# First FFN projection: products added in PSUM, two tiles begun together, differences on VectorE

## The chip, the cores and the metric

The kernel runs on one core of a Trainium2 chip (trn2). A core has a matrix engine (TensorE, PE in the profile; its weight loads are PEld), three engines for elementwise work (VectorE, DVE; ScalarE, ACT; GpSimd, POOL), SyncE (SP), which here issues most DMAs, and DMA engines. The engines run side by side, each through its own queue in order, and wait for each other on semaphores. The metric is the device time of one execution in microseconds (us); lower is better.

## What is computed

The reference is one encoder layer in float32: windowed attention with 16 heads over 2048 tokens of width 1024, then a SwiGLU feed-forward network (FFN) with a hidden width of 2816, each between norms and gates. The stage that the change edits is the first line of the FFN:

```python
def swiglu(h, w_in, w_out):
    a, b = jnp.split(h @ w_in, 2, axis=-1)
    return (jax.nn.silu(a) * b) @ w_out
```

## The kernel before

**Stages.** Attention comes first, then from about 780 us on the first FFN projection (`h @ w_in`, silu, product), from about 1645 us the second (`@ w_out`), with the last norm and gate at the end. Results of the first projection go to DRAM and are read back by the second.

**Precision.** Every float32 operand is split into a high and a low half (`split`, L149: a cast on ACT writes the high half, L150; a subtraction on DVE writes the low one, L151), and each product is three matmuls (`three`, L143: high x high, high x low, low x high).

**Seven products for eight.** The first projection works on two halves of 1024 tokens (`hf`), each two chunks of 512 tokens, and on 22 tiles of hidden columns (`t`), each 128 columns of `a` and the matching 128 of `b`. A tile is a 2 x 2 block product of weights (a11, a12, a21, a22) and tokens (b11, b12, b21, b22), computed in Winograd's form: seven products of sums s1 to s4 of the weights (on POOL, L879 to L882) with sums t1 to t4 of the tokens (made earlier, and read from DRAM). A product (`Block.step`) is 4 steps of depth x 3 = 12 matmuls of 128 x 512 into one PSUM bank; a tile is 84 matmuls. The names in the profile are pc_i for the banks, wa_i and ws_i for the split weights, hb and ht for the split tokens, wiri for the raw weights, s_i for their sums.

**What reads the banks.** The order of products is `STEPS` with `OPERANDS`: b11, t2, b21, t3, t1, t4, b22. Each product has a bank of its own, six banks turn around (`psC`, L825). `Hidden.take` (L939 to L963) reads each bank once, the fifth twice, and adds them up in SBUF tiles: p1 (a copy by ACT, L943), u2, u3, b1 (additions by DVE, L946 to L962). `done` takes the silu of each `a` block on ACT (L968) and multiplies it by its `b` block on POOL (L972).

**Pairs.** After each odd tile `give_pair` writes the two tiles' results to DRAM, with the sums that the second projection needs: two subtractions on POOL (L923, L927), two on DVE (L924, L930). In the second half (`parted`, the parts in `SPLIT`) it splits each result before writing (gh and gl tiles), and its last two tiles are written without sums.

**Around it.** `Operands.load` reads and splits the tokens of a half; four of the seven operands of the first half can be loaded only when the attention's last blocks have freed their memory, the first three earlier. Weights of a tile go through one of two raw tiles (`wi`), and their splits through two rings of 7 (`ww`). `late_h` prepares the tokens of the last chunks (transposes, L659, and differences, L676 to L683) between the tiles of the first half. The last two tiles of each half go product by product in turn (`interleaved`), while the next half's operands, or the second projection's first operands (`first_weights`), are loaded.

**What sets the order.** The framework plans each engine's queue ahead: it goes through the instructions by the order of the program (with a few raised in priority), by their dependences and its own estimate of their times. On the chip an engine then works through its queue in that order, and an instruction that waits holds what stands behind it.

Of the kernel before, what the change touches and what calls it, by code (L numbers as in the profile page):

```python
# [17 lines left out]
P = 128  # L18
# [49 lines left out]
def encoder_layer(ctx, tc, a):  # L68
# [71 lines left out]
    def rot(pl, tag, bufs):  # L140
        return lambda name: pl.tile([P, CH], F32, tag=tag, name=name, bufs=bufs)

    def three(ps, w, h, first=False, last=False):  # L143

        pe.matmul(ps, w[0], h[0], start=first, stop=False)  # L145
        pe.matmul(ps, w[0], h[1], start=False, stop=False)  # L146
        pe.matmul(ps, w[1], h[0], start=False, stop=last)  # L147

    def split(hi, lo, src, eng):  # L149
        act.copy(hi, src)  # L150
# [714 lines left out]

    class Block:

        STEPS = tuple(zip(("a11", "s2", "a12", "s3", "s1", "a22", "s4"), OPERANDS))

        def __init__(self, ops, i, u, wa, wb):  # L870
            self.ops, self.u, m = ops, u, ops.m
# [9 lines left out]
            pool.tensor_tensor(sm_["s3"], a11, a21, ALU.subtract)  # L881
            pool.tensor_tensor(sm_["s4"], a12, sm_["s2"], ALU.subtract)  # L882
            src = dict(sm_, a11=a11, a12=a12, a22=a22)
            self.w = {}
            for e, (n, _) in enumerate(self.STEPS):
                side = int(e >= 3 and ww[1] is not None)
                w = ww[side].tile([P, 2, m, P], F32R, tag="w", bufs=wbufs[side], name=f"w{n}_{u}")
                split(w[:, 0], w[:, 1], src[n], dve)
                self.w[n] = w

        def step(self, i):
            an, bn = self.STEPS[i]
            w, h, m = self.w[an], self.ops.ops[bn], self.ops.m
# [7 lines left out]
    def give_pair(hf, j):  # L901

        b = {f"b{e + 1}{i + 1}": hidden.pop((2 * j + e, i)) for e in range(2) for i in range(CPH)}
        parted = (hf, part_of[hf][j][0]) in SPLIT

        def give(n, t, keep):
            d = g_d[hf][j][n]
            if not parted:
                sp.dma_start(d[:, 0], t)
                return  # L910
            hi = temp(f"gh{hf}_{j}_{n}").bitcast(F32R)
            lo = (temp(f"gl{hf}_{j}_{n}") if keep else t).bitcast(F32R)
# [12 lines left out]
        give("t3", b12, False)  # L925
        give("b22", b22, True)
        pool.tensor_tensor(b22, b22, b11, ALU.subtract)  # L927
        give("t1", b11, False)
        give("b21", b21, True)
        dve.tensor_tensor(b21, b21, b22, ALU.subtract)  # L930
        give("t2", b22, False)
        give("t4", b21, False)

    class Hidden(Block):
        def __init__(self, half, t, hf):
            super().__init__(half, t, f"i{half.u}_{t}", a["w_in"][t], a["w_in"][HT + t])
            self.t, self.got, self.hf = t, {}, hf

        def take(self, i, ps):  # L939
            u = self.u  # L940
            if i == 0:
                self.p1 = temp(f"p1_{u}")
                act.copy(self.p1, ps)  # L943
            elif i == 1:
                self.u2 = temp(f"u2_{u}")
                dve.tensor_tensor(self.u2, ps, self.p1, ALU.add)  # L946
# [18 lines left out]
        def done(self, i, j, v):  # L965

            if i == 0:
                act.activation(v, v, AF.Silu)  # L968
            self.got[i, j] = v
            if (1 - i, j) in self.got:  # L970
                sa, b = self.got[0, j], self.got[1, j]
                pool.tensor_tensor(sa, sa, b, ALU.mult)  # L972
                hidden[self.t, j] = sa
                if self.t % 2 and len(self.got) == 4:
                    give_pair(self.hf, self.t // 2)

    def interleaved(pair, nxt, end=iter(())):
# [10 lines left out]
    def first_weights():  # L988

        raws, m = [], PARTS[0][0]  # L990
        for k in range(m):
            raws.append([hA.tile([P, 2, CH], F32R, tag="b11", name=f"wr0_{k}_{e}") for e in range(2)])
            for e in range(2):
                sp.dma_start(f(raws[k][e]), a["w_out"][2 * k + e].rearrange("p (i c) -> p i c", i=2))
        yield
        for k in range(m):
# [6 lines left out]
        for i in range(2):  # L1003
            for k in range(m):
                t = b21p.tile([P, 2, CH], F32R, tag="b21", name=f"g0_{i}_{k}")
                sp.dma_start(f(t[:, 1]), g_d[0][k][("b21", "t1")[i]][:, 0])
                split(t[:, 0], t[:, 1], f(t[:, 1]), dve)
                first_g[0, 0, i, k] = t
        yield
        for i, n in enumerate(("a12", "s1", "a11")):  # L1010
            for k, src in enumerate(first_src):
                t = t3p.tile([P, 2, CH], F32R, tag="t3" if i < 2 else "t1", name=f"wo0_{n}_{k}")
                split(t[:, 0], t[:, 1], src[n], dve)
                first_w[0, 0, i, k] = t
                if n == "s1":
                    pool.tensor_tensor(src["s2"], src["s1"], src["a11"], ALU.subtract)
                    pool.tensor_tensor(src["s4"], src["a12"], src["s2"], ALU.subtract)
            if i == 1:
                yield
# [37 lines left out]
                        h2_d[hf * CPH + int(n[2]) - 1][:, 2 * k + (n[1] == "2"), :])  # L1057
    half = half_ops(0)
    with tc.high_priority(offset=1):
        half.load("b11", "t2", "b21")  # L1060
    last_blocks(range(LAG, JB))
    held = Hidden(half, 0, 0)
    st0.close()
# [3 lines left out]
    wi[1] = open_pool(ffn, "wi1")  # L1067
    ww[1] = open_pool(ffn, "ww1")
    with tc.high_priority(offset=100):
        half.load("t3", "t1", "t4", "b22")  # L1070
    tmp = open_pool(ffn, "tmp", 10)
    cbp = open_pool(ffn, "cbp", 2)

# [12 lines left out]

    gating = gate()
    for hf in range(S // HALF):
        for t in range(HT - 2):
            hid = Hidden(half, t, hf) if held is None else held  # L1090
            held = None
            for i in range(7):
                hid.step(i)
            next(gating if hf else late, None)
        pair = [Hidden(half, t, hf) for t in range(HT - 2, HT)]
        half = None
        if hf + 1 < S // HALF:
# [71 lines left out]
    class Grams:  # L1169
# [4 lines left out]
        def load(self, n=1):  # L1174
            for _ in range(n):
# [4 lines left out]
                for k in range(PARTS[hf][p]):  # L1180
# [4 lines left out]
                        latest[:] = [sp.dma_start(f(t), d).ins]  # L1185
                    else:
                        latest[:] = [sp.dma_start(f(t[:, 1]), d[:, 0]).ins]
                        split(t[:, 0], t[:, 1], f(t[:, 1]), dve)
                    self.g[hf, p, i, k] = t

    z = {}
# [160 lines left out]
```

## Time and profile before

| | us |
|---|---|
| median of 3 runs | 2087.45 |
| lowest, highest | 2087.05, 2092.54 |
| the profiled execution | 2086.54 |
| its span | 2084.7 |

The span is the stretch from the first to the last instruction that the profile shows. Durations come from this one execution. A row of a timeline gives start, duration, engine, line, operation, output <- input, partitions x elements and count, and in brackets how long the engine was idle before it and what it waited for. A row of waits gives the total in us, the count and the longest. Matmul records last 0.39 us and overlap; their starts tell the rate.

### The profile page before, as it was taken

To read this page: it belongs to the slowest core of one execution; us is meant where nothing else is said; L and a number is where in the kernel's file an instruction comes from. 1 tells how busy PE (TensorE), PEld (TensorE's weight loads), DVE (VectorE), ACT (ScalarE), POOL (GpSimd) and SP (SyncE) were. 2 spreads that over 40 slices of the span, in tenths; PEclk is the share of its full clock that TensorE was granted. 3 is DMA by queue.
4 is the path that set the end of the run, shared out by engine and by line. 5 is a ranking of instruction groups with operands and counts; after the bars stand their busy time and mean duration, and the time that the engine had idled before them with its cause. 6 is when DMAs were issued, how large, how long until landed. Compare 5 with 4: busy or idle time off the path is not lost.

```text
span 2084.7 us, 28731 instructions
## 1 busy us (share of the span) xinstructions
PE 2011.4 (96%) x9416; PEld 1660.3 (80%) x9416; DVE 1505.5 (72%) x2629; ACT 994.7 (48%) x2105; POOL 912.5 (44%) x894
## 2 busy tenths in 40 slices
PE   8698999999999998999999999999999999999998
PEld 5576787888888786888888887888888788888886
DVE  7376677677777668566576698787876598887656
ACT  4233677777777756333333353434433544453222
POOL 0412456543446536455666455545553333344300
PEclk9899999999999999999999999999999999999999
DMA  8699668665556665433643454544533454488763
GB/s 313 194 284 289 199 190 254 177 168 179 179 175 211 206 230 202 141 121 122 228 171 113 154 183 152 198 156 144 200 137 142 161 174 145 156 307 339 258 251 122
DMA packets 257285, 402.69 MB, mean 193 GB/s; under 512 B 84661, under 2 KB 135397, under 8 KB 255088
## 3 DMA queue, kind: packets, MB, share of 16 engines
q1 hardware_dynamic: 216592, 371.41, 52.9%
q10 hardware_dynamic: 39072, 25.18, 3.9%
q0 software_dynamic: 1472, 4.27, 0.5%
q8 instruction: 74, 1.21, 0.2%
q14 instruction: 75, 0.61, 0.1%
HBM read 267.83 MB, written 132.95 MB: 192 GB/s over the span
## 4 chain that ended last, share of the span: by engine, by line
PE 42%; DVE 4%; DMA 1%; issue 1%; POOL 1%; ACT 1%; SPq 0%; DVEq 0%; ACTq 0%; POOLq 0%
PE pc_i L145 8%; PE pc_i L147 8%; PE pc_i L146 8%; PE po L1205 5%; PE po L1206 5%; PE po L1204 5%; DVE z L1245 1%; PE pl L1229 1%; PE pl L1227 1%; PE pl L1228 1%; DMA wiri<-w_in 0%; DVE z L1249 0%; DMA ht<-hd_d_t 0%; DVE z L1209 0%; DVE wo_s L151 0%
## 5 line engine op out<-in xcount | busy, mean ns | idle before, releaser
L146 PE MATMUL pc_i<-ht,ws_i 128*128 128x512 f32 x528 | 207.1, 392 | 1.6 <-DVE ht L151 1.6
L145 PE MATMUL pc_i<-ht,ws_i 128*128 128x512 f32 x528 | 206.2, 391 | 1.8 <-ACT ht L150 1.7
L147 PE MATMUL pc_i<-ht,ws_i 128*128 128x512 f32 x528 | 206.8, 392 | 0.0
L150 ACT CAST wa_i<-wiri 128x512 fp32r<-128x512 f32 x132 | 81.7, 620 | 218.3 <-DMA wiri<-w_in 115.3
L507 POOL TENSOR_SCALAR pr<-pr,rs 128x288 f32<-128x288 f32 (+3 forms) x256 | 126.4, 514 | 116.3 <-DVE rs L505 106.5
L501 DVE CUSTOM_DVE_ANT_0 pr<-s,bias,nsink 128x288 f32<-128x288 f32 (+3 forms) x256 | 124.2, 500 | 57.5 <-PE s L498 47.3
L503 ACT ACTIVATE pr<-pr,nm 128x289 f32<-128x289 f32 (+3 forms) x256 | 135.3, 531 | 55.9 <-DVE nm L501 54.3
L879 POOL TENSOR_TENSOR s_i<-wiri 128x512 f32<-128x512 f32 x44 | 63.9, 1453 | 193.4 <-DMA wiri<-w_in 176.3
L151 DVE TENSOR_TENSOR wa_i<-wiri,wa_i 128x512 fp32r<-128x512 f32 x132 | 127.9, 969 | 22.3 <-ACT wa_i L150 22.0
L151 DVE TENSOR_TENSOR ws_i<-s_i,ws_i 128x512 fp32r<-128x512 f32 x132 | 125.4, 950 | 22.0 <-ACT ws_i L150 21.8
L1209 DVE TENSOR_TENSOR z<-po,z 128x512 f32<-128x512 f32 x164 | 110.6, 684 | 42.2 <-PE po L1206 40.4
L145 PE MATMUL pc_i<-hb,wa_i 128*128 128x512 f32 x352 | 138.1, 392 | 0.0
L147 PE MATMUL pc_i<-hb,wa_i 128*128 128x512 f32 x352 | 137.7, 391 | 0.0
L151 DVE TENSOR_TENSOR plo<-t,phi 128x512 fp32r<-128x512 f32 x184 | 121.9, 683 | 21.9 <-ACT phi L150 21.7
L146 PE MATMUL pc_i<-hb,wa_i 128*128 128x512 f32 x352 | 137.5, 391 | 0.0
L1204 PE MATMUL po<-wo_s,g 128*128 128x512 f32 x320 | 124.8, 393 | 2.0 <-DVE z L1209 1.4
L498 PE MATMUL s<-k,q 128*128 128x288 f32 (+4 forms) x512 | 110.0, 313 | 16.7 <-DMA k<-k_d 10.4
L1205 PE MATMUL po<-wo_s,g 128*128 128x512 f32 x320 | 125.4, 392 | 0.1
L1206 PE MATMUL po<-wo_s,g 128*128 128x512 f32 x320 | 125.2, 391 | 0.0
L520 PE MATMUL t<-ident,pr 128*128 128x128 f32 x736 | 116.0, 274 | 3.1 <-POOL pr L507 2.7
L145 PEld LDWEIGHTS pc_i<-ht,ws_i 128*128 128x128 f32 x528 | 99.5, 188 | 24.1 <-ACT ht L150 2.2
L146 PEld LDWEIGHTS pc_i<-ht,ws_i 128*128 128x128 f32 x528 | 99.5, 188 | 23.6 <-DVE ht L151 2.1
(251 smaller groups left out, 5907.2 us busy)
## 6 DMA issues: line engine op xcount, KB each, us to landing
wiri<-w_in SPq DMA_DIRECT2D x88, 512.0 KB, 4.7
ada<-ada_w SPq DMA_DIRECT2D x40, 512.0 KB, 6.4
wr<-w_out SPq DMA_DIRECT2D x20, 1024.0 KB, 9.1
g<-g_d_t SPq DMA_DIRECT2D x36, 512.0 KB, 5.2
g<-g_d_b SPq DMA_DIRECT2D x35, 512.0 KB, 5.7
q<-q_d SPq DMA_DIRECT2D x16, 1024.0 KB, 6.6
wsr<-w_qkv SPq DMA_DIRECT2D x24, 512.0 KB, 5.7
g<-g_d_t SPq DMA_DIRECT2D x44, 256.0 KB, 3.0
```

What stands on the lines that cost most here:

```text
L145: pe.matmul(ps, w[0], h[0], start=first, stop=False)
L146: pe.matmul(ps, w[0], h[1], start=False, stop=False)
L147: pe.matmul(ps, w[1], h[0], start=False, stop=last)
L151: return eng.tensor_tensor(lo, src, f(hi), ALU.subtract).ins
L501: dve.tensor_tensor_reduce(pr[:, i, lo:hi], ps[:, :n], bias[g][:, lo - starts[i]:hi - starts[i]], -1.0, nsink[:, g:g + 1], ALU.add, ALU.mi ...
L503: act.activation(pr[:, i, lo:hi + 1], pr[:, i, lo:hi + 1], AF.Exp, bias=nm[:, i:i + 1], scale=-1.0, accum_out=rs[:, i:i + 1])
L507: pool.tensor_scalar(pr[:, i, lo:hi], pr[:, i, lo:hi], rs[:, i:i + 1], 1.0, ALU.mult, ALU.mult)
L520: pe.transpose(pt[:, i * P:(i + 1) * P], pr[:, i, jj * P:(jj + 1) * P], ident)
L1204: pe.matmul(ps, g[:, 0], w[:, 0], start=i < FRESH and k == 0, stop=False, **on)
L1205: pe.matmul(ps, g[:, 0], w[:, 1], start=False, stop=False, **on)
L1206: pe.matmul(ps, g[:, 1], w[:, 0], start=False, stop=k == m - 1, **on)
L1209: dve.tensor_tensor(y, ps, y, ALU.add)
```

## The change

- **Products and banks.** The order becomes a11 b11, a12 b21, s2 t2, s1 t1, s3 t3, s4 b22, a22 t4, and `CHAIN` gives each product a bank: 0, 1, 0, 3, 0, 3, 0. Products 2, 4 and 6 add to the bank of product 0, product 5 to that of product 3, after the bank has been read. A tile uses three banks.
- **Reads.** ACT copies after products 0, 2 and 3 (y11, y12, y22); DVE adds the bank to y11, y22, y12 after products 1, 4 and 5, and multiplies y11 by it after product 6. Silu of y11 comes after product 1, of y12 after product 5; POOL keeps one product per tile.
- **Start.** In the first half, products 0 to 2 of tile 0 and of tile 1 come first, then 3 to 6 of each.
- **Pairs.** In the second half the two POOL subtractions of a pair go to DVE. In the second projection two stages' splits go from DVE to POOL.
- The loads and the early operands of the second projection follow the new order of operands.

```diff
-OPERANDS = ("b11", "t2", "b21", "t3", "t1", "t4", "b22")
+OPERANDS = ("b11", "b21", "t2", "t1", "t3", "b22", "t4")
...
-        STEPS = tuple(zip(("a11", "s2", "a12", "s3", "s1", "a22", "s4"), OPERANDS))
+        STEPS = tuple(zip(("a11", "a12", "s2", "s1", "s3", "s4", "a22"), OPERANDS))
+        CHAIN = (0, 1, 0, 3, 0, 3, 0)
...
-            ps = psC.tile([P, CH], F32, tag="p", name=f"pc{i}_{self.u}")
+            fresh = self.CHAIN[i] == i
+            if fresh:
+                self.bank[i] = psC.tile([P, CH], F32, tag="p", name=f"pc{i}_{self.u}")
+            ps = self.bank[self.CHAIN[i]]
             for k in range(m):
-                three(ps, (w[:, 0, k], w[:, 1, k]), h[k], k == 0, k == m - 1)
+                three(ps, (w[:, 0, k], w[:, 1, k]), h[k], fresh and k == 0, k == m - 1, not fresh)
...
+        eng = dve if parted else pool
         give("b11", b11, True)
-        pool.tensor_tensor(b11, b12, b11, ALU.subtract)
+        eng.tensor_tensor(b11, b12, b11, ALU.subtract)
...
-        pool.tensor_tensor(b22, b22, b11, ALU.subtract)
+        eng.tensor_tensor(b22, b22, b11, ALU.subtract)
...
             if i == 0:
-                self.p1 = temp(f"p1_{u}")
-                act.copy(self.p1, ps)
+                self.y11 = temp(f"y11_{u}")
+                act.copy(self.y11, ps)
             elif i == 1:
-                self.u2 = temp(f"u2_{u}")
-                dve.tensor_tensor(self.u2, ps, self.p1, ALU.add)
+                dve.tensor_tensor(self.y11, ps, self.y11, ALU.add)
+                act.activation(self.y11, self.y11, AF.Silu)
             elif i == 2:
-                dve.tensor_tensor(self.p1, ps, self.p1, ALU.add)
-                self.done(0, 0, self.p1)
+                self.y12 = temp(f"y12_{u}")
+                act.copy(self.y12, ps)
             elif i == 3:
-                self.u3 = temp(f"u3_{u}")
-                dve.tensor_tensor(self.u3, ps, self.u2, ALU.add)
+                self.y22 = temp(f"y22_{u}")
+                act.copy(self.y22, ps)
             elif i == 4:
-                dve.tensor_tensor(self.u2, ps, self.u2, ALU.add)
-                b1 = temp(f"b1_{u}")
-                dve.tensor_tensor(b1, ps, self.u3, ALU.add)
-                self.done(1, 1, b1)
+                dve.tensor_tensor(self.y22, ps, self.y22, ALU.add)
             elif i == 5:
-                dve.tensor_tensor(self.u3, ps, self.u3, ALU.add)
-                self.done(1, 0, self.u3)
+                dve.tensor_tensor(self.y12, ps, self.y12, ALU.add)
+                act.activation(self.y12, self.y12, AF.Silu)
+                pool.tensor_tensor(self.y12, self.y12, self.y22, ALU.mult)
+                hidden[self.t, 1] = self.y12
             else:
-                dve.tensor_tensor(self.u2, ps, self.u2, ALU.add)
-                self.done(0, 1, self.u2)
...
+                dve.tensor_tensor(self.y11, ps, self.y11, ALU.mult)
+                hidden[self.t, 0] = self.y11
...
+        if held is not None:
+            held = [held, Hidden(half, 1, hf)]
+            for r in (range(3), range(3, 7)):
+                for hid in held:
+                    for i in r:
+                        hid.step(i)
+            for hid in held:
+                next(late, None)
...
-                        split(t[:, 0], t[:, 1], f(t[:, 1]), dve)
+                        split(t[:, 0], t[:, 1], f(t[:, 1]), pool if (hf, p) == (0, 0) and i in (3, 4) else dve)
```

More of the change, by code (lines that the diff above doesn't have):

```diff
@@ L141, in rot, with three @@
         return lambda name: pl.tile([P, CH], F32, tag=tag, name=name, bufs=bufs)
[L143 to L147, printed above, removed]
+    def three(ps, w, h, first=False, last=False, on=False):
+        pe.matmul(ps, w[0], h[0], start=first, stop=False, skip_group_check=on)
+        pe.matmul(ps, w[0], h[1], start=False, stop=False, skip_group_check=on)
+        pe.matmul(ps, w[1], h[0], start=False, stop=last, skip_group_check=on)
     def split(hi, lo, src, eng):
@@ L866, in encoder_layer @@
     class Block:
-        STEPS = tuple(zip(("a11", "s2", "a12", "s3", "s1", "a22", "s4"), OPERANDS))
+        STEPS = tuple(zip(("a11", "a12", "s2", "s1", "s3", "s4", "a22"), OPERANDS))
+        CHAIN = (0, 1, 0, 3, 0, 3, 0)
         def __init__(self, ops, i, u, wa, wb):
-            self.ops, self.u, m = ops, u, ops.m
+            self.ops, self.u, m, self.bank = ops, u, ops.m, {}
             pl = wi[(i + 1) % 2 if i or ops.u != "0" else 0]
@@ L936, in __init__ @@
             super().__init__(half, t, f"i{half.u}_{t}", a["w_in"][t], a["w_in"][HT + t])
-            self.t, self.got, self.hf = t, {}, hf
+            self.t, self.hf = t, hf
         def take(self, i, ps):
@@ L941, in take @@
             if i == 0:
-                self.p1 = temp(f"p1_{u}")
-                act.copy(self.p1, ps)
+                self.y11 = temp(f"y11_{u}")
+                act.copy(self.y11, ps)
             elif i == 1:
-                self.u2 = temp(f"u2_{u}")
-                dve.tensor_tensor(self.u2, ps, self.p1, ALU.add)
+                dve.tensor_tensor(self.y11, ps, self.y11, ALU.add)
+                act.activation(self.y11, self.y11, AF.Silu)
             elif i == 2:
-                dve.tensor_tensor(self.p1, ps, self.p1, ALU.add)
-                self.done(0, 0, self.p1)
+                self.y12 = temp(f"y12_{u}")
+                act.copy(self.y12, ps)
             elif i == 3:
-                self.u3 = temp(f"u3_{u}")
-                dve.tensor_tensor(self.u3, ps, self.u2, ALU.add)
+                self.y22 = temp(f"y22_{u}")
+                act.copy(self.y22, ps)
             elif i == 4:
-                dve.tensor_tensor(self.u2, ps, self.u2, ALU.add)
-                b1 = temp(f"b1_{u}")
-                dve.tensor_tensor(b1, ps, self.u3, ALU.add)
-                self.done(1, 1, b1)
+                dve.tensor_tensor(self.y22, ps, self.y22, ALU.add)
             elif i == 5:
-                dve.tensor_tensor(self.u3, ps, self.u3, ALU.add)
-                self.done(1, 0, self.u3)
-            else:
-                dve.tensor_tensor(self.u2, ps, self.u2, ALU.add)
-                self.done(0, 1, self.u2)
[L965 to L974, printed above, removed]
+                dve.tensor_tensor(self.y12, ps, self.y12, ALU.add)
+                act.activation(self.y12, self.y12, AF.Silu)
+                pool.tensor_tensor(self.y12, self.y12, self.y22, ALU.mult)
+                hidden[self.t, 1] = self.y12
+            else:
+                dve.tensor_tensor(self.y11, ps, self.y11, ALU.mult)
+                hidden[self.t, 0] = self.y11
+                if self.t % 2:
                     give_pair(self.hf, self.t // 2)
@@ L995, in first_weights @@
         yield
+        for i in range(2):
+            for k in range(m):
+                t = b21p.tile([P, 2, CH], F32R, tag="b21", name=f"g0_{i}_{k}")
+                sp.dma_start(f(t[:, 1]), g_d[0][k][("b21", "t1")[i]][:, 0])
+                split(t[:, 0], t[:, 1], f(t[:, 1]), dve)
+                first_g[0, 0, i, k] = t
+        yield
         for k in range(m):
@@ L1002, in first_weights @@
         yield
[L1003 to L1006, printed above, removed]
-                split(t[:, 0], t[:, 1], f(t[:, 1]), dve)
-                first_g[0, 0, i, k] = t
-        yield
         for i, n in enumerate(("a12", "s1", "a11")):
             for k, src in enumerate(first_src):
-                t = t3p.tile([P, 2, CH], F32R, tag="t3" if i < 2 else "t1", name=f"wo0_{n}_{k}")
+                t = t3p.tile([P, 2, CH], F32R, tag="t1" if i < 2 else "t3", name=f"wo0_{n}_{k}")
                 split(t[:, 0], t[:, 1], src[n], dve)
@@ L1059, in encoder_layer @@
     with tc.high_priority(offset=1):
-        half.load("b11", "t2", "b21")
+        half.load("b11", "b21", "t2")
     last_blocks(range(LAG, JB))
@@ L1069, in encoder_layer @@
     with tc.high_priority(offset=100):
-        half.load("t3", "t1", "t4", "b22")
+        half.load("t1", "t3", "b22", "t4")
     tmp = open_pool(ffn, "tmp", 10)
@@ L1088, in encoder_layer @@
     for hf in range(S // HALF):
-        for t in range(HT - 2):
-            hid = Hidden(half, t, hf) if held is None else held
-            held = None
+        if held is not None:
[6 more added lines that the diff above has]
+                next(late, None)
+        for t in range(2 if held is not None else 0, HT - 2):
+            hid = Hidden(half, t, hf)
             for i in range(7):
@@ L1094, in encoder_layer @@
             next(gating if hf else late, None)
+        held = None
         pair = [Hidden(half, t, hf) for t in range(HT - 2, HT)]
```

1 line of the change is left out of this document (removed).

## The prediction

> **What bounds the kernel now.** I read the page first, then busy time by stretches, then the list of who waited for whom.
>
> ```profile
> span 2084.7 us, 28731 instructions
> PE 2011.4 (96%) x9416; PEld 1660.3 (80%) x9416; DVE 1505.5 (72%) x2629; ACT 994.7 (48%) x2105; POOL 912.5 (44%) x894
> ```
>
> TensorE (PE) works 96% of the span, no other engine above 72%. In the stage that the change edits, only time in which PE stands still, or runs at its slow clock, can be won. The stretches (columns: stretch, length, then PE, PEld, DVE, ACT, POOL busy with counts, granted clock, DMA share, GB/s):
>
> ```profile
> 1300.00:1350.00 50.00, 50.00 (x221) 41.15 (x220) 38.29 (x51) 21.25 (x37) 27.36 (x20) 1.00 0.51 189
> 780.00:830.00 50.00, 42.75 (x172) 33.94 (x171) 42.24 (x69) 31.25 (x59) 29.08 (x18) 0.93 0.62 220
> 1259.00:1284.00 25.00, 22.38 (x92) 17.97 (x91) 22.21 (x28) 9.24 (x17) 15.30 (x11) 0.93 0.56 200
> 1657.00:1670.00 13.00, 11.48 (x40) 8.30 (x39) 12.31 (x21) 10.01 (x19) 0.00 (x0) 0.87 0.41 136
> ```
>
> The first row is the steady state: 221 matmuls in 50 us, 0.226 us each at clock 1.00, so a product (12 matmuls) takes 2.71 us and a tile (7 products) 19.0 us. The other rows are the three holes of the stage: its start (172 matmuls where 221 fit: 49 x 0.226 = 11.1 us lost), the third tile of the second half (92 for 110.5: 4.2 us), and the first products of the second projection (40 for 57.5: 4.0 us). Together **19.3 us**: the most that the change can win here. What makes the holes:
>
> ```profile
> PE pc_i L145 <- ACT p_i L943: 6.6, 2, 4.0
> PE pc_i L145 <- ACT ht L150: 1.7, 1, 1.7
> PE pc_i L146 <- DVE ht L151: 1.6, 1, 1.6
> PE po L1204 <- DVE z L1209: 1.4, 2, 0.7
> 1277.66 0.80 PE L145 MATMUL pc_i<-hb,ws_i 128*128 128x512 f32 x1 [2.62 <-ACT p_i L943]
> 1278.25 0.63 PE L146 MATMUL pc_i<-hb,ws_i 128*128 128x512 f32 x1
> 1278.68 0.63 PE L147 MATMUL pc_i<-hb,ws_i 128*128 128x512 f32 x1
> ```
>
> PE waited for operand splits (ht), for z additions, and twice for a bank that the copy L943 had not read. The last rows show a second price: after 2.62 us of idling the matmuls start 0.43 us apart, not 0.226. The hole of 4.2 us is 2.6 of waiting and 1.6 of slow matmuls; I price any long wait so.
>
> **The change, part by part.** *Work on the side engines.*
>
> ```profile
> L943 ACT COPY p_i<-pc_i x44: 566/578/590, 806.1 to 1613.1; 128x512 f32<-128x512 f32 x44
> L946 DVE TENSOR_TENSOR u_i<-pc_i,p_i x44: 676/679/692, 807.5 to 1618.6; 128x512 f32<-128x512 f32 x44
> L972 POOL TENSOR_TENSOR p_i<-p_i,u_i x44: 1293/1734/2271, 819.9 to 1641.1; 128x512 f32<-128x512 f32 x44
> L927 POOL TENSOR_TENSOR u_i<-u_i,p_i x20: 1285/1297/1742, 845.6 to 1577.4; 128x512 f32<-128x512 f32 x20
> L930 DVE TENSOR_TENSOR p_i<-p_i,u_i x20: 1177/1771/1790, 846.9 to 1580.4; 128x512 f32<-128x512 f32 x20
> L151 DVE TENSOR_TENSOR gl_b<-p_i,gh_b x18: 677/692/1780, 1259.0 to 1575.0; 128x512 fp32r<-128x512 f32 x18
> 1388.53 1.73 POOL L881 TENSOR_TENSOR wiri<-wiri 128x512 f32<-128x512 f32 x1
> 1389.04 1.77 DVE L930 TENSOR_TENSOR p_i<-p_i,u_i 128x512 f32<-128x512 f32 x1
> ```
>
> A tile now has seven DVE reads of accumulators (L946 to L962); after it four: 3 x 0.68 = 2.0 us of DVE less per tile, 90 us over 44 tiles. One POOL product of two per tile goes (1.7 x 44 = 76 us). ACT gets two copies more (1.2 x 44 = 51 us). All of it lies beside a busy PE, so it is worth nothing by itself; what it changes is how late these engines are. PE does the same 84 matmuls a tile, with the same weights; adding to a bank already written is what 11 of 12 matmuls of a product do now, at the same 0.226 us, so I put no cost on it.
>
> In the second half the pairs move two subtractions each from POOL to DVE. L927 took 1.3 us on POOL. On DVE, two inputs from SBUF took 0.69 us or 1.77 us (gl_b and L930: the median of the one is the maximum of the other): 18 moved operations are 12 to 32 us of DVE, also off the path. The long ones stand beside running POOL operations, as the last two rows do. The Trainium skill ("SBUF — State Buffer", Who interferes with whom) says that a VectorE instruction with two SBUF inputs contends with a GpSimd instruction that reads SBUF and that the second to issue blocks fully; by it these would cost the 32 us, and not 12, wherever POOL makes the weight sums at that time.
>
> *The start.* PE has the first six products (two tiles by three) before it needs the fourth operand: from 780.71 that is 780.7 + 6 x 2.71 = 797.0. In the old order it came there after three, and its first split (ht) kept PE until 792.87. Those two waits go. What is late next (engine rows: start, duration):
>
> ```profile
> 780.71 0.39 PE L145 MATMUL pc_i<-hb,wa_i 128*128 128x512 f32 x1
> 792.87 0.80 PE L146 MATMUL pc_i<-ht,ws_i 128*128 128x512 f32 x1 [1.55 <-DVE ht L151]
> 790.67 0.61 ACT L150 CAST wa_i<-wiri 128x512 fp32r<-128x512 f32 x1
> 806.12 0.58 ACT L943 COPY p_i<-pc_i 128x512 f32<-128x512 f32 x1
> 792.73 0.69 DVE L151 TENSOR_TENSOR wa_i<-wiri,wa_i 128x512 fp32r<-128x512 f32 x1
> ```
>
> The second tile's first weights are split at 790.67 and 792.73, ready at 793.4. PE has done three products of the first tile at 788.8, so it waits 4.6 us and pays 1.6 for the slow clock: 6.2 lost instead of 11.1, a gain of 4.9. That needs the first copy at 783.4; before, it came at 806.12. If it stays there, PE stops after two products (786.1), goes on at 793.4 with two of the second tile and the fourth product of both (fresh banks, to 804.2), then waits to 806.7: 7.3 + 2.5 + 2 x 1.6 = 13.0, a loss of 1.9. I take **-2**: the weights' row is fixed by the attention's last blocks, which the change leaves alone; the copy's row is one that the new order makes early.
>
> *The half boundary.* The wait of 2.62 us was for a copy that stood in ACT's queue behind casts of the pair's differences. The differences are now all on DVE and DVE has less to do; gain 0 to 4.2, I take **-3**.
>
> *The second projection.*
>
> ```profile
> 1658.11 3.10 DVE L151 TENSOR_TENSOR g<-g 128x512 fp32r<-128x512 f32 x5 [0.58 <-ACT g L150]
> 1661.32 1.29 DVE L1209 TENSOR_TENSOR z<-po,z 128x512 f32<-128x512 f32 x2
> ```
>
> Five splits of 0.6 us stand on DVE ahead of the z additions for which PE waits (2 x 0.7, plus 2.6 of slow matmuls). Four splits (two stages of two tiles) go to POOL, idle in that stretch (0.00 in the row of 1657 to 1670): z can come up to 2.4 us earlier, and the wait of 1.4 is shorter than that. Two POOL operations at once could make DVE splits long (1.77). Gain 0 to 4.0; I take **-3**.
>
> *The added wait.* A bank is now written again two products after it was read: product 2 waits for the copy of product 0, 4 for 2, 5 for 3, and 6 for DVE's addition of product 4. Before, six banks gave 16 us. How late were these reads?
>
> ```profile
> 1380.25 0.39 PE L147 MATMUL pc_i<-hb,wa_i 128*128 128x512 f32 x1
> 1383.20 0.39 PE L145 MATMUL pc_i<-hb,wa_i 128*128 128x512 f32 x1
> 1390.89 0.62 ACT L150 CAST gh_t<-p_i 128x512 fp32r<-128x512 f32 x1 [2.92 <-DVE p_i L930]
> 1391.42 0.58 ACT L943 COPY p_i<-pc_i 128x512 f32<-128x512 f32 x1
> ACT gh_t L150 <- DVE p_i L930: 26.7, 9, 3.3
> DVE h L677 <- POOL ld L676: 22.5, 4, 6.5
> ```
>
> Product 0 ended at 1380.6, product 2 starts at 1383.2, and the copy began at 1391.42, because ACT's queue held a cast that waited for L930. In the new order PE would have stood from 1383.2 to 1392.0, 8.8 us; this happened in 9 tiles: 9 x (8.8 + 1.6) = 94 us, the far end. The near end is 0: the copies get other places in ACT's queue, since the order of each queue is planned with the dependences known; L930's own wait was for POOL's L927, which is on DVE now; and ACT is busy 21.25 of 50 us. Below nothing it cannot go. I take **0**, by the three reasons, and keep a part of the far end as a rival. The weights' loads also move: a22 becomes the last weight cast, so the raw tile is free, and the next load on SP issued, some products later; loads run two tiles ahead (38 us) and landed in 4.7 us (median of the page), so nothing.
>
> Sum: the profiled execution took 2086.5 (span 2084.7 and 1.8 around it); -2 -3 -3 +0 = 2078.5. The median of the runs is 0.9 above it: **2079**.
>
> **The rivals.** *Slower: the reads stay late in the second half.* After each odd tile of the second half, the pair's differences, splits and casts (some 11 DVE operations) run while POOL makes weight sums. At 1.77 us instead of 0.69 the chain falls some 4 us behind its plan, and the copies of the next tile stand behind its casts. Decisive is whether product 0's copy ends 2.7 us (one product) after the product; 2 us more is a wait of 2 + 1.6 us in 9 tiles: +32, 2111. For it: the 10.8 us of lateness above, and 1.77 as the median of L930. Against: POOL's part of that chain is gone. The same rule is in the Trainium skill ("PSUM — Partial Sum Buffer", Summary: rules for kernel authors), which advises a different bank for reading while matmuls run; this change gives that distance away, and no run here shows yet what it costs.
>
> *No difference: given back.* The holes shrink, but four tiles of the first half (the row of L677: DVE held 22.5 us in 4 waits for POOL and a load) now hold the silu of product 1, and ACT's copy of product 2 behind it: 4 x 2 us, about 2087.
>
> *All three holes go*: copies early and no new wait, 2086.5 - 19.3 + 0.9 = 2068.
>
> **How the numbers follow.** Forecast (2072 to 2081) 0.36; all holes 0.14; given back 0.20; late reads 0.30. A measurement of this kernel tells about 0.3% (6.3 us) from no change. Faster than 2081: the first two, 0.50. Within: 0.20. Slower than 2094: 0.30. The range reaches from below the second case to just past the late reads' price, 2066 to 2112, and leaves out lateness near the 94 us; the likeliest case alone is 2072 to 2081.
>
> **What would show it.** Right: 780 to 830 with more than 172 matmuls, the stretches of the other two holes at full count, and no group of waits of pc_i on ACT's copies or DVE's additions in steady tiles. Wrong: PE waits for the y12, y22 or y11 copies, at clock below 1.00, tile after tile; or a first copy near 806 again. If steady windows of 50 us hold fewer than 221 matmuls after odd tiles of the second half, the late reads have it.

## The result and the profile after

| | before | changed kernel |
|---|---|---|
| median of the runs (us) | 2089.73 (4 runs, 2087.05 to 2092.54) | 2122.62 (4 runs, 2120.08 to 2127.26) |
| span of the profiled execution (us) | 2084.7 | 2122.3 |
| first projection, first to last matmul (us) | 864.6 | 895.4 |
| part of the span behind it (us) | 439.4 | 440.0 |

The change makes the kernel slower: the ratio is 1.016, with a 95% interval of 1.0134 to 1.0185. The forecast was 2079 and the range ended at 2112. Of the 37.6 us between the two spans, 30.8 lie in the first projection. It began 6.2 us later (786.9 for 780.7); that is the scatter of the attention ahead of it, since in the other kernels below it began between 780.1 and 791.6 and the order of TensorE's matmuls up to there is the same in both.

The head of the changed kernel's page, and its busy time by stretches (stretch, length, PE, PEld, DVE, ACT, POOL with counts, granted clock, DMA share, GB/s):

```profile
span 2122.3 us, 28456 instructions
...
PE 2025.2 (95%) x9416; PEld 1660.9 (78%) x9416; DVE 1432.4 (67%) x2511; ACT 1041.0 (49%) x2193; POOL 836.0 (39%) x836
```

```profile
786.00:836.00 50.00, 37.80 (x143) 28.65 (x142) 37.21 (x57) 31.55 (x63) 19.98 (x15) 0.86 0.63 222
1300.00:1350.00 50.00, 49.14 (x215) 39.88 (x214) 33.26 (x46) 22.10 (x40) 18.05 (x12) 1.00 0.54 180
```

VectorE has 73 us less to do and POOL 76, as the count of instructions said. TensorE does the same 9416 matmuls. The first row covers the 50 us from the stage's start: 143 matmuls, where the same stretch of before had 172. The second, from 1300 us, is where the kernel before ran steadily: 215 for 221, with one of the waits below in it. Who waited for whom (total us, times, longest):

```profile
PE pc_i L145 <- ACT y_i L948: 13.0, 10, 2.9
PE pc_i L145 <- ACT wa_i L150: 5.8, 1, 5.8
PE pc_i L145 <- DVE y_i L950: 4.1, 1, 4.1
PE pc_i L145 <- ACT y_i L954: 2.9, 2, 1.8
PE po L1206 <- DVE z L1211: 2.8, 3, 1.3
```

L948 is ACT's copy of product 0: TensorE waits for it ten times, once at the stage's start and nine times in even tiles of the second half. Cut into stretches of 84 matmuls (a tile's worth), the stage shows where the time went. Each figure is worked out from the starts of the matmuls in the trace:

| stretch (us) | before | changed | difference |
|---|---|---|---|
| first two tiles | 49.8 | 58.0 | +8.1 |
| tile 12 of the first half | 20.0 | 22.7 | +2.7 |
| tiles 0 and 1 of the second half | 38.3 | 45.3 | +7.0 |
| tile 2 of the second half | 23.5 | 19.3 | -4.2 |
| even tiles 4 to 18 of the second half, each | 19.14 | 20.4 to 21.6 | +12.7 in all |
| other tiles, each | 19.14 (steady) | 19.3 | +4.4 in all |

Tile 20 of the second half has no such wait. The code writes the last four tiles of that half without sums (the part `LAST` has two pairs), not the last two as described above, so no pair's differences stand ahead of tile 20; the pairs of tiles 0 to 17 make the nine that the prediction counts.

### The profile page after: what moved, and what is told of

The parts are those of the page before. It is cut to its first block, busy times and chain, and to the rows that moved or that the text cites. A ratio compares the mean times of both kernels' runs of the same rounds, so it can differ in the third digit from the quotient of the medians.

```text
span 2122.3 us, 28456 instructions
## 1 busy us (share of the span) xinstructions
PE 2025.2 (95%) x9416; PEld 1660.9 (78%) x9416; DVE 1432.4 (67%) x2511; ACT 1041.0 (49%) x2193; POOL 836.0 (39%) x836
## 4 chain that ended last, share of the span: by engine, by line
PE 28%; issue 8%; DVE 7%; POOL 3%; DMA 2%; ACT 2%; SPq 0%; ACTq 0%; DVEq 0%; POOLq 0%
PE po L1207 5%; PE po L1208 5%; PE po L1206 5%; PE pc_i L145 4%; PE pc_i L147 4%; PE pc_i L146 4%; POOL y_i L963 1%; DVE ws_i L151 1%; POOL s_i L880 1%; POOL s_i L881 1%; DMA wiri<-w_in 1%; DVE z L1247 1%; PE pl L1230 1%; PE pl L1229 1%; DMA ht<-hd_d_t 1%
## 5 line engine op out<-in xcount | busy, mean ns | idle before, releaser
L151 DVE TENSOR_TENSOR wa_i<-wiri,wa_i 128x512 fp32r<-128x512 f32 x132 | 108.0, 831 | 97.9 <-ACT wa_i L150 97.7
L150 ACT CAST ws_i<-s_i 128x512 fp32r<-128x512 f32 x132 | 81.4, 619 | 147.5 <-PE pc_i L147 101.6
L145 PE MATMUL pc_i<-hb,wa_i 128*128 128x512 f32 x352 | 140.8, 400 | 9.9 <-ACT wa_i L150 5.8
L147 PE MATMUL pc_i<-hb,wa_i 128*128 128x512 f32 x352 | 139.6, 396 | 0.8 <-DVE wa_i L151 0.8
L146 PE MATMUL pc_i<-hb,wa_i 128*128 128x512 f32 x352 | 139.9, 397 | 0.0
L1211 DVE TENSOR_TENSOR z<-po,z 128x512 f32<-128x512 f32 x164 | 110.7, 684 | 42.5 <-PE po L1208 40.8
L145 PEld LDWEIGHTS pc_i<-ht,ws_i 128*128 128x128 f32 x528 | 99.3, 188 | 45.9 <-ACT y_i L948 18.3
```

The costliest lines, as they stand in the source:

```text
L145: pe.matmul(ps, w[0], h[0], start=first, stop=False, skip_group_check=on)
L146: pe.matmul(ps, w[0], h[1], start=False, stop=False, skip_group_check=on)
L147: pe.matmul(ps, w[1], h[0], start=False, stop=last, skip_group_check=on)
L151: return eng.tensor_tensor(lo, src, f(hi), ALU.subtract).ins
```

## The experiments

My first theory was that the reads of reused banks come late; the rivals were the start, the pairs and, later, the weights. The times of all runs, each with the ratio to before on the same chip:

| run | median (us) | ratio, 95% interval | first projection | even tiles 4 to 18, mean |
|---|---|---|---|---|
| e1_one_start | 2120.52 | 1.0151 [1.0132, 1.0171] | 892.0 | 20.75 |
| e2_fresh_banks | 2118.81 | 1.0147 [1.0125, 1.0170] | 890.2 | 21.12 |
| e3_pool_pairs | 2121.56 | 1.0148 [1.0125, 1.0170] | 895.0 | 20.63 |
| e4_before_pairs | 2088.87 | 1.0002 [0.9990, 1.0013] | 859.5 | 19.14 |
| f1_a22_early | 2156.50 | 1.0334 [1.0316, 1.0351] | 932.1 | 26.21 |
| f2_fresh_a22_early | 2094.15 | 1.0042 [1.0027, 1.0058] | 865.5 | 19.51 |
| f3_before_a22_late | 2116.98 | 1.0150 [1.0135, 1.0165] | 893.6 | 21.79 |
| g1_pairs_behind_copy | 2112.55 | 1.0109 [1.0089, 1.0129] | 883.8 | 20.59 |
| g2_before_second | 2092.02 | 1.0018 [1.0006, 1.0030] | 863.9 | 19.14 |
| g3_pairs_second | 2086.84 | 0.9997 [0.9985, 1.0009] | 860.0 | 19.14 |
| h1_sums_on_dve | 2139.55 | 1.0223 [1.0202, 1.0244] | 914.1 | 24.17 |

**One tile after the other at the start** (e1), the changed kernel without its two-tile start:

```diff
-        if held is not None:
-            held = [held, Hidden(half, 1, hf)]
...
-        for t in range(2 if held is not None else 0, HT - 2):
-            hid = Hidden(half, t, hf)
+        for t in range(HT - 2):
+            hid = Hidden(half, t, hf) if held is None else held
+            held = None
```

> The changed kernel with one part undone: tile 0 runs all seven products before tile 1, as before. In the changed kernel the first two tiles took 58.0 us (49.8 before), the whole first projection 895.4 us from its first to its last matmul (864.6 before). Theory A, the reads of reused banks are the cost and the two-tile start is neither gain nor loss: the first two tiles stay within 3 us of 58, the total within 5 us of 2123, because the third product of tile 0 now waits for the first copy, which came 28 us after the stage began. Rival B, the two-tile start itself costs the 8 us: the first two tiles return to about 50 and the total to about 2115.

The first two tiles took 56.4 us instead of 58.0, still 6.6 above before. The two-tile start is neither the gain that I forecast nor the cause of the loss.

**A bank for each product** (e2), the changed kernel with the additions on VectorE again:

```diff
-        CHAIN = (0, 1, 0, 3, 0, 3, 0)
+        CHAIN = (0, 1, 2, 3, 4, 5, 6)
...
             elif i == 2:
-                self.y12 = temp(f"y12_{u}")
-                act.copy(self.y12, ps)
+                dve.tensor_tensor(self.p1, ps, self.p1, ALU.add)
...
```

> The changed kernel with the accumulation undone: order of products, two-tile start and differences on VectorE stay, but every product has a bank of its own and VectorE adds them (eight reads of banks and one copy a tile, and again two GpSimd products). Theory A, the waits for reads of reused banks cost most of the 31 us of the stage: the waits in even tiles of the second half (1.1 to 2.3 us each) and the 7 us in its first two tiles go, a plain tile falls from 19.3 to 19.14 us, and the stage falls from 895 to 864 to 873; total 2088 to 2100. Rival B, order, start or the differences on VectorE cost it: the stage stays above 885 and the total near 2120.

The steady tiles went back to exactly 19.14 us, so the 0.15 to 0.2 us more of each, some 7 us over the stage, comes with the reused banks (the last section shows by what way). But the even tiles stayed slow, at 20.1 to 22.0, and tile 2 of the second half took 26.8. With six banks to go round, TensorE still waited for product 0's copy. My first theory, as the account of the whole loss, fell here.

**The pairs on POOL again** (e3), the changed kernel with `eng = pool` for all pairs:

> The changed kernel with one part undone: both subtractions of a pair are back on GpSimd in the second half. Theory A, the copy of product 0 stands behind the casts of the pair, so it gets later by the GpSimd operations and what they wait for: the wait in each even tile of the second half grows from 1.2 us to 3 to 9 us, the total by 15 to 70 us, to 2140 to 2190. Rival B, the subtractions on VectorE beside GpSimd's weight sums are what makes the copies late: the waits shrink below 0.5 us and the total falls by about 10 us, to 2113.

Even tiles at 20.2 to 21.1, the time within 1.1 us of the changed kernel's: who makes the differences does not decide, and neither theory had the right size.

**The pairs on VectorE in the kernel before** (e4):

```diff
+        eng = dve if parted else pool
...
-        pool.tensor_tensor(b11, b12, b11, ALU.subtract)
+        eng.tensor_tensor(b11, b12, b11, ALU.subtract)
...
-        pool.tensor_tensor(b22, b22, b11, ALU.subtract)
+        eng.tensor_tensor(b22, b22, b11, ALU.subtract)
```

> The kernel before with one part of the change alone: the pair's two GpSimd subtractions of the second half on VectorE. The hole in the third tile of the second half (23.55 us instead of 19.14) came from a copy behind casts of such a pair. Theory A: that hole goes and nothing else changes, total 3 to 5 us below before, 2085. Rival B: VectorE, full from 1200 to 1250 us, falls further behind and the hole stays or grows: total as before or up to 5 us above.

The first projection took 5.1 us less: tile 2 of the second half went from 23.5 to 20.1 us. Tile 0 of the first half went from 30.3 to 28.9, but it lies ahead of the edit, which changes the second half alone: that part is scatter, and 3.5 us are the edit's. The total did not follow beyond its scatter (ratio 1.0002).

What the slow kernels had in common was the new order of the products, and with it the place of a22. A tile's raw weights (`raw`) are free for the next load but one when their last reader is done, and that is the split of a22. In the list that the loop goes through, splits 3 to 6 of a tile share seven slots (`wbufs`, `side`). The split issued sixth takes the slot that the last product of two tiles before held; the split issued seventh takes that of the fourth product of the tile before. Moving a22 from sixth to seventh place therefore delays its split by up to four products, 10.9 us, and the load behind it. The landing of the loads shows it: in tiles 4 to 18 of the second half the weights land 47 to 52 us ahead of the tile's 84 matmuls in the kernel before, and 36 to 41 in the changed one. POOL, whose weight sums wait for the load, waits longer, though in part because it has less to do. Its waits, first before, then changed:

```profile
POOL s_i L879 <- DMA wiri<-w_in: 176.3, 38, 19.6
```

```profile
POOL s_i L880 <- DMA wiri<-w_in: 378.0, 40, 22.6
```

Three runs tested it.

**a22 split sixth in the changed kernel** (f1), the products in their new order:

```diff
-            for e, (n, _) in enumerate(self.STEPS):
+            for e, n in enumerate(("a11", "a12", "s2", "s1", "s3", "a22", "s4")):
```

> The changed kernel with one edit: the split of weights a22 is issued sixth, before that of s4, instead of last; the products keep their order. Theory C (late weights): a raw weight tile is free when a22, its last part, is split. With seven slots for the last four splits of a tile, a split issued seventh must wait for the slot that the fourth product of the tile before frees; issued sixth it waits for one that was free four products (10.9 us) earlier. So in the changed kernel the next load, the POOL sums and the splits come late, splits that wait for their DMA stand in ACT's queue ahead of the copies, and the even tiles of the second half lose 12.7 us. C expects these tiles at 19.2 to 19.6 us instead of 20.4 to 21.6, and a time of 2106 to 2113 us. Rival (late reads of reused banks): the even tiles stay above 20.3 us and the time stays at 2119 to 2125.

**The same edit with a bank for each product** (f2):

> The kernel in which every product has a bank of its own again (new product order, start and pairs kept), with the split of a22 issued sixth. In that kernel without this edit the plain tiles took 19.14 us, the even tiles of the second half 20.1 to 22.0, its third tile 26.8. Theory C: even tiles 19.1 to 19.5, third tile below 23.6, a time of 2095 to 2104 us. Rival (the new order of products itself delays the reads, whatever the weights do): even tiles stay above 20.0, 2115 to 2122 us.

**a22 split seventh in the kernel before** (f3):

```diff
-            for e, (n, _) in enumerate(self.STEPS):
+            for e, n in enumerate(("a11", "s2", "a12", "s3", "s1", "s4", "a22")):
```

> The kernel before with one edit: the split of a22 is issued seventh, after that of s4; products, banks and pairs are those of before. It adds the suspected cost alone. Theory C: the raw tile is released four products later, weights come late, the even tiles of the second half go from 19.14 to 20 us or more (10 to 20 us in all), and the time goes to 2098 to 2112 us. Rival (a22's place does not matter without the new order of products): 2087 to 2092 us, even tiles at 19.1 to 19.2.

f3 is the cleanest: one line, no bank reused, no new order of products, and the kernel before takes 29.0 us more in its first projection (893.6 for 864.6); its weights land 35 to 41 us ahead, as late as in the changed kernel. At 2116.98 it was even slower than the 2112 that theory C allowed. The loss is nearly as large as the change's, but f1 below shows that the change's 30.8 us can't be put down to the weights alone. f2 is the other side: early weights give back 24.7 us of e2 (865.5 for 890.2), and six of its eight even tiles are at 19.14; the time, 2094.15, is just below the 2095 to 2104 expected and still 0.3 to 0.6% above the kernel before. My account of the path was not exact, though. I had put the copies behind splits that wait for their DMA; the traces show a detour over POOL. First e2, then f2, around the start of tile 8 of the second half (1391.6 and 1381.2; start, duration, engine, line):

```profile
1394.49 1.29 POOL L880 TENSOR_TENSOR s_i<-wiri 128x512 f32<-128x512 f32 x1 [6.84 <-DMA wiri<-w_in]
...
1399.14 1.74 POOL L965 TENSOR_TENSOR y_i<-y_i,y_i 128x512 f32<-128x512 f32 x1
...
1400.92 1.76 DVE L929 TENSOR_TENSOR y_i<-y_i,y_i 128x512 f32<-128x512 f32 x1 [1.19 <-POOL y_i L965]
...
1408.91 0.62 ACT L150 CAST gh_t<-y_i 128x512 fp32r<-128x512 f32 x1 [1.91 <-DVE y_i L935]
1409.44 0.58 ACT L948 COPY p_i<-pc_i 128x512 f32<-128x512 f32 x1
```

```profile
1377.30 1.30 POOL L880 TENSOR_TENSOR s_i<-wiri 128x512 f32<-128x512 f32 x1 [3.91 <-DMA wiri<-w_in]
...
1383.90 1.51 POOL L965 TENSOR_TENSOR y_i<-y_i,y_i 128x512 f32<-128x512 f32 x1 [0.19 <-ACT y_i L964]
...
1386.49 0.68 DVE L929 TENSOR_TENSOR y_i<-y_i,y_i 128x512 f32<-128x512 f32 x1
...
1396.26 0.58 ACT L948 COPY p_i<-pc_i 128x512 f32<-128x512 f32 x1 [0.69 <-DMA g_d_b<-gh_b]
```

With late weights POOL's sums begin 2.9 us after the tile's start, and POOL's multiplication of the odd tile's y12 by y22 (L965), for which the pair waits, stands behind them. The first of the pair's subtractions that needs the odd tile (L929; L928 needs the even tile alone) starts 9.3 us after the tile's start instead of 5.3, the casts follow, and the next copy stands behind those: 17.8 us instead of 15.1. In f2 the casts ahead of the copy waited for DMAs that still read their buffers, and the copy was early enough even so. Product 6 needs that bank six products after the start, at 16.3 us. One copy is in time, the other is not.

f1, against both of its theories, was slower by 34 us than the changed kernel. The holes of tile 12 and of tiles 0 and 1 of the second half did go (20.3 us, 38.9 in all), but the even tiles rose to 25.7 to 26.8. The same place of the pair (tile 8 in the changed kernel, engine by engine):

```profile
1417.60 0.69 DVE L151 TENSOR_TENSOR wa_i<-wiri,wa_i 128x512 fp32r<-128x512 f32 x1
1418.20 0.69 DVE L151 TENSOR_TENSOR y_i<-y_i,gh_t 128x512 fp32r<-128x512 f32 x1
1418.80 0.69 DVE L151 TENSOR_TENSOR gl_b<-y_i,gh_b 128x512 fp32r<-128x512 f32 x1
...
1420.29 0.62 ACT L150 CAST gh_t<-y_i 128x512 fp32r<-128x512 f32 x1 [1.91 <-DVE y_i L935]
1420.82 0.58 ACT L948 COPY y_i<-pc_i 128x512 f32<-128x512 f32 x1
...
1427.90 1.28 POOL L880 TENSOR_TENSOR s_i<-wiri 128x512 f32<-128x512 f32 x1 [14.12 <-DMA wiri<-w_in]
...
1421.45 0.50 PE L145 MATMUL pc_i<-ht,ws_i 128*128 128x512 f32 x1 [1.24 <-ACT y_i L948]
```

and in f1:

```profile
1415.23 1.78 DVE L151 TENSOR_TENSOR wa_i<-wiri,wa_i 128x512 fp32r<-128x512 f32 x1
1416.93 1.78 DVE L151 TENSOR_TENSOR y_i<-y_i,gh_t 128x512 fp32r<-128x512 f32 x1
1418.63 1.76 DVE L151 TENSOR_TENSOR gl_b<-y_i,gh_b 128x512 fp32r<-128x512 f32 x1
1420.32 1.75 DVE L151 TENSOR_TENSOR wa_i<-wiri,wa_i 128x512 fp32r<-128x512 f32 x1
...
1422.74 0.62 ACT L150 CAST gh_t<-y_i 128x512 fp32r<-128x512 f32 x1 [2.97 <-DVE y_i L935]
1423.27 0.58 ACT L948 COPY y_i<-pc_i 128x512 f32<-128x512 f32 x1
...
1416.53 1.62 POOL L881 TENSOR_TENSOR s_i<-s_i,wiri 128x512 f32<-128x512 f32 x1
...
1423.90 0.80 PE L145 MATMUL pc_i<-ht,ws_i 128*128 128x512 f32 x1 [4.78 <-ACT y_i L948]
```

In both, the copy stands directly behind the pair's last cast. In the changed kernel POOL stands still for 14.12 us, waiting for late weights, and VectorE's splits take 0.69 us. In f1 the weights are there, POOL makes its sums just then, and the same splits take 1.75 to 1.78 us; the copy falls behind, and TensorE waits 4.78 us instead of 1.24. So late weights also hid the price of the reused banks. Two more runs tested the two parts of this.

**A pair's casts behind the next copy** (g1), f1 with the pair issued later:

```diff
-                act.copy(self.y11, ps)
+                got = act.copy(self.y11, ps).ins
+                if pending:
+                    with tc.issue_after(got):
+                        give_pair(*pending.pop())
...
-                if self.t % 2:
+                if self.t == HT - 1:
                     give_pair(self.hf, self.t // 2)
+                elif self.t % 2:
+                    pending.append((self.hf, self.t // 2))
```

> The changed kernel with a22's split issued sixth (2156 us, even tiles of the second half at 25.7 to 26.8 us), and a pair's differences issued only behind the next tile's first copy, so that their casts stand behind that copy in ACT's queue. Theory D: in that kernel PE waits in nine tiles 4.4 us for a copy that stands behind casts which wait for VectorE's differences; with six slots of slack (a bank for each product) the same queue cost nothing, with a reused bank each wait counts, and 1.6 to 2 us of slow matmuls come behind it. D expects the even tiles at 19.3 to 20.3 us, and 2096 to 2108 us. Rival (adding into a bank just read is slow for another reason, or the reads on VectorE are what is late): even tiles above 23 us, 2140 to 2157 us.

44 us come back (2156.50 to 2112.55), and six of the eight even tiles are below 20.9; the waits for copy L948 shrink from 39.5 us in all to 1.1, all of it at the stage's start. The time misses the expected 2108 by 4.5 us, and only three of the eight even tiles lie in the expected 19.3 to 20.3. Product 6 now waits for VectorE's addition of product 4 (L962, 6.8 us in five waits), and one tile took 23.0. Each time the addition stands behind VectorE operations of 1.5 to 1.8 us; at tile 8 they run beside POOL's sums:

```profile
1387.54 1.77 DVE L151 TENSOR_TENSOR wa_i<-wiri,wa_i 128x512 fp32r<-128x512 f32 x1
1389.23 1.76 DVE L928 TENSOR_TENSOR y_i<-y_i,y_i 128x512 f32<-128x512 f32 x1
1390.91 0.68 DVE L962 TENSOR_TENSOR y_i<-pc_i,y_i 128x512 f32<-128x512 f32 x1
...
1388.72 1.72 POOL L883 TENSOR_TENSOR s_i<-wiri,s_i 128x512 f32<-128x512 f32 x1
...
1391.64 0.50 PE L145 MATMUL pc_i<-ht,wa_i 128*128 128x512 f32 x1 [1.82 <-DVE y_i L962]
```

The place of the copy in ACT's queue is what made f1 slow; the late reads on VectorE, which the rival named, are what is left.

**The weight sums on VectorE** (h1), f1 in its second half:

```diff
-            pool.tensor_tensor(sm_["s1"], a21, a22, ALU.add)
+            adder = dve if ops.u == "1" else pool
+            adder.tensor_tensor(sm_["s1"], a21, a22, ALU.add)
...
```

> The changed kernel with a22's split issued sixth (2156 us, even tiles of the second half at 25.7 to 26.8 us), and in the second half the four weight sums of a tile on VectorE instead of POOL. In that kernel VectorE's splits of a pair's differences took 1.75 us each beside POOL's sums, four of them in a row; where POOL waited for late weights, in the changed kernel itself, the same splits took 0.69 us and PE waited 1.24 us instead of 4.78. Theory E (two engines at once make VectorE's splits long, and that makes the copy late): without sums on POOL the splits take 0.69 us, the copy comes up to 4 us earlier, even tiles at 19.3 to 22.5 us, 2105 to 2130 us. Rival (only the order of the queues counts; the sums, 4 x 0.69 us more on VectorE, stand ahead of the differences): even tiles at 24.5 us or more, 2145 to 2160 us.

```profile
1416.74 0.68 DVE L151 TENSOR_TENSOR gl_b<-y_i,gh_b 128x512 fp32r<-128x512 f32 x1
1417.34 0.68 DVE L151 TENSOR_TENSOR y_i<-y_i,gh_t 128x512 fp32r<-128x512 f32 x1
...
1418.54 0.68 DVE L884 TENSOR_TENSOR s_i<-wiri,s_i 128x512 f32<-128x512 f32 x1
1419.14 0.68 DVE L936 TENSOR_TENSOR y_i<-y_i,y_i 128x512 f32<-128x512 f32 x1
...
1421.06 0.79 PE L145 MATMUL pc_i<-ht,ws_i 128*128 128x512 f32 x1 [3.24 <-ACT y_i L949]
```

The time, 2139.55, lies between the theories, and the even tiles (22.9 to 25.2) fit neither. Without POOL's sums the splits take 0.68 us, so what made them long was the other engine; but the sums (4 x 0.68) now stand ahead of the pair's last difference (L936) and take back most of that. Both count. This edit gave back 2.0 us an even tile, the casts behind the copy (g1) 5.6; what the long splits cost by themselves the run doesn't tell, because the sums are in the way.

**The second projection's start alone** (g2), the kernel before with that edit, and **with the pairs on VectorE** (g3):

```diff
-                        split(t[:, 0], t[:, 1], f(t[:, 1]), dve)
+                        split(t[:, 0], t[:, 1], f(t[:, 1]), pool if (hf, p) == (0, 0) and i in (3, 4) else dve)
```

> The kernel before with the change's edits of the second projection's start alone: four splits of its products 4 and 5 on POOL, the first G tiles loaded ahead of the first weight sums. Theory of the prediction: the part behind the first projection goes from 439.4 to 436.4 us, 3 us less in all. Rival (POOL's splits are long and others late in their place): that part stays at 439 to 442 us, the time within 2 us of before.

> The kernel before with two parts of the change: the pair differences of the second half on VectorE (the first projection took 859.5 us with them, 864.6 without) and the second projection's start of the run beside it. Theory: the first projection at 858 to 861 us; if the second projection gains its 3 us, 2079 to 2083 us in all, otherwise 2083 to 2088 us. Rival (VectorE's added work gives back later what the projection wins): no faster than before, 2087 to 2090 us.

In g2 the part behind the first projection took 440.2 us, before 439.4, and the kernel as a whole was slower by 0.06 to 0.3%. Its VectorE and POOL there:

```profile
1657.92 5.51 POOL L151 TENSOR_TENSOR g<-g 128x512 fp32r<-128x512 f32 x4 [6.99 <-ACT g L150]
...
1661.20 3.39 DVE L151 TENSOR_TENSOR g<-g 128x512 fp32r<-128x512 f32 x3 [3.15 <-ACT g L150]
1664.51 1.27 DVE L1209 TENSOR_TENSOR z<-po,z 128x512 f32<-128x512 f32 x2
```

VectorE has three splits left ahead of the z additions where it had five, but beside POOL's they take 1.13 us each instead of 0.62, 3.39 in all for 3.10, and they begin later, behind ACT's casts. TensorE's waits for z grow from 1.4 us in all to 2.3. g3 keeps the shorter first projection (860.0) and has 439.1 behind it; its ratio, 0.9997, holds no gain that can be told from none. No version tried beats the kernel before.

## Why the prediction was wrong

**What bounds the kernel** was read rightly: the work taken from VectorE and POOL bought nothing by itself.

**The weights' loads** are the step that failed. I put a22's new place, "the next load on SP issued, some products later", at nothing, because loads run two tiles ahead and land in 4.7 us. I looked at the load alone, which still lands 35 to 41 us ahead. Behind it come POOL's sums, ahead of the pair's products in POOL's queue, and these set when the pair's casts let the next copy through. f3 shows the price of this step by itself, +29.0 us.

**The added wait**, which I took as 0, also failed, and would have cost more without the first error. The first projection in the new order of products, in us:

| | weights early | weights late |
|---|---|---|
| a bank for each product | 865.5 (f2) | 890.2 (e2) |
| reused banks | 932.1 (f1) | 895.4 (changed) |

With early weights, reused banks cost 66.6 us; with late ones 5.2. Each alone costs, and the two don't add up, so the 30.8 us of the change can't be divided between them. My rival "the reads stay late" named the place, the queue and VectorE beside POOL, and f1 shows it as described, at nearly twice its price: 6.7 us more in an even tile than f2's, to the 3.6 that I reckoned. The Trainium skill ("SBUF — State Buffer", Who interferes with whom) has a VectorE instruction with two SBUF inputs contend with a GpSimd instruction that reads SBUF; the trace agrees, 1.75 to 1.78 us beside POOL's sums and 0.68 to 0.69 without, for the same splits. In the changed kernel itself that rival was held down by POOL's idle 14.12 us. The reason "the order of each queue is planned" did not hold: the planned order put the copy behind casts that came late.

**No cost for adding into a used bank** held for the adding itself (last section). What I left out is that reused banks change the order of TensorE's queue: 0.15 to 0.2 us a tile, some 7 us.

**The start**, -2, became +8.1. The wait for the second tile's weights came as reckoned (5.77 us for 4.6), but behind it stood more:

```profile
798.36 0.80 PE L145 MATMUL pc_i<-hb,wa_i 128*128 128x512 f32 x1 [5.77 <-ACT wa_i L150]
...
822.93 0.80 PE L145 MATMUL pc_i<-hb,wa_i 128*128 128x512 f32 x1 [4.15 <-DVE y_i L950]
...
815.14 0.57 ACT L948 COPY y_i<-pc_i 128x512 f32<-128x512 f32 x1
```

The first copy came at 815.14, even later after the stage's start than in the kernel before; the case that I priced at +1.9 held, and then VectorE's addition was waited for as well. So the price of that case, too, was too low. Of the 8.1 us, 1.6 go with the two-tile start (e1) and 3.2 with late weights in the pair of runs with own banks (55.5 to 52.3). What is left of the comparison is not additive: f1, with early weights and used banks, has 59.1.

**The half boundary**, -3, was right in kind and size (-4.2 in tile 2; e4 shows -3.5 from the pairs alone), but tiles 0 and 1 before it lost 7.0. Early weights (f1) or own banks (e2) each take most of that back, to 38.9 and 39.5 us where before has 38.3; f3, late weights on the old order, has 42.5.

**The second projection**, -3, became +0.6, which is within the scatter (e4, with the second projection of before, has 438.2 for 439.4). The splits moved as planned; what I named in passing, that POOL makes VectorE's splits long, took the gain.

## What to carry to other kernels

Before reordering work that goes through rings of slots, work out for each slot which earlier use frees it: one place later in a list of splits freed a buffer four products later here, and cost 29 us. A buffer's distance hides a badly ordered queue; where a change gives the distance away, put the reads ahead of whatever in that queue waits for another engine. Test two suspects in all four combinations: here each of them could be taken for the cause, mending the banks alone (e2) changed little, and mending the weights alone (f1) made the kernel slower.

## What was not expected of the hardware

**Which waits cost more than themselves.** The stretch of 20 us around the waits shown above, first in the changed kernel (1.24 us of waiting), then in f1 (4.78):

```profile
1410.00:1430.00 20.00, 18.76 (x82) 14.97 (x81) 13.94 (x21) 9.74 (x18) 5.61 (x5) 1.00 0.71 235
```

```profile
1410.00:1430.00 20.00, 15.22 (x59) 11.97 (x58) 14.31 (x17) 8.09 (x15) 7.62 (x5) 0.83 0.65 236
```

82 matmuls at clock 1.00 stand against 59 at 0.83. Between such lengths the length alone does not decide. Two stretches of f3, with a wait of 2.43 us in the first and of 2.41 us in the second:

```profile
1450.00:1470.00 20.00, 17.57 (x71) 14.08 (x70) 15.64 (x24) 7.19 (x13) 8.57 (x7) 0.91 0.59 203
1574.00:1594.00 20.00, 17.59 (x78) 14.24 (x77) 15.12 (x25) 7.01 (x14) 8.13 (x6) 1.00 0.54 184
```

I worked out, for all kernels, what tiles 2 to 19 of the second half with a single wait lost beyond the wait and their steady 19.14 or 19.29 us. It was 0.2 to 0.6 us for every wait up to 1.5 us, 1.5 to 2.7 us for every wait from 3.5 us on, and either of the two between 1.8 and 3.4 us. The 1.6 us that I had put on any long wait is right for f1's waits, and too much for those of the changed kernel, 0.9 to 1.5 us long.

**Adding into a used bank is free, changing over is not.** The last 84 matmuls of the first half are products 3 to 6 of its last two tiles. In the changed kernel 72 of them add into banks that have been read; they start 226.7 ns apart and the 84 take 19.05 us, just as in the kernel before and in e2. What takes time is going over between a tile's first three products and its last four, whose weights come from different rings and whose tokens from different buffers. After each such change the next ten or so matmuls start up to 236 ns apart. With a bank for each product the queue has two changes in a tile. In every kernel with reused banks, products of neighbouring tiles stand interleaved in it, and a steady tile of the first half has six. No change and 19.05 us, two and 19.14, six and 19.34: about 0.05 us for each. Whether the weights' ring or the tokens' buffer makes it is open, since both change together.
